# The end of layer 0: factor transposes among the last values' products, weight splits behind the values and behind six heads

## The chip, the cores and the metric

The kernel runs on one core of one Trainium2 chip. The metric is the device time in microseconds, the median of several runs. Before the change the median of three runs was 1199.51 us (1198.51 to 1203.9).

## What is computed

A transformer encoder of two layers over 512 tokens of width 1024, all in float32. Each layer is RMSNorm, a token mixer, a residual add, then RMSNorm, a squared-ReLU MLP of width 4096, a residual add; a final RMSNorm follows. Layer 0 mixes with dilated windows, layer 1 with differential attention. The change lies at the end of layer 0's mixer, which in the reference is:

```python
for (win, dil, nh) in A_GROUPS:          # ((128, 1, 6), (512, 4, 5), (2048, 16, 5))
    ...
    o, lse = lax.map(block_fn, (qb, starts))     # windowed softmax attention, o = p @ v
    glses.append(jax.nn.logsumexp(lse, axis=-1) - math.log(nh))
alpha = jax.nn.softmax(jnp.stack(glses, axis=-1), axis=-1)
o = jnp.concatenate([outs[g] * (n_groups * alpha[..., g])[..., None, None] ...], axis=2)
return o.reshape(B, S, A_HEADS * HEAD_DIM) @ w_o
```

So each of the 16 heads' outputs is multiplied, token by token, by a factor (its group's share, and here also one over its softmax sum), and the result is multiplied by the projection `w_o`.

## The kernel before

**Products in three parts.** Activations are kept with features on the partitions, 128 x 512 tiles. To hold float32 accuracy, each operand of a large product is split into a high half, rounded to the matmul's format by a copy on ScalarE (`whi`, L157, or `oh`, L693), and a low half, the rest, by a subtraction on VectorE (`wlo`, L158, or `ol`, L694). `mm3` (L168 to L170) then issues three products of 512 columns: high by high, high weight by low activation, low weight by high activation.

**Weights.** A unit of weights is 1024 x 256 and is fetched by SyncE into `raw`; its split is made in two halves of columns. `raw`, `whi` and `wlo` have two buffers each. `next_w()` hands out the unit fetched earlier and fetches and splits the one after it: one unit ahead. So the step that opens the last values splits the projection's first unit, and the step that opens the projection splits its second unit.

**Steps.** `linear_steps` is a generator: each `next` issues one `mm3` (one of eight blocks of the contraction), and after eight steps the result of one block of 128 output features, here one pair of heads, goes to `on_out`. `values0(j)` gives the values of pairs 2j and 2j + 1: for each pair 24 products into a bank `acc`, the scaling by VectorE (v, L554, remembered as `scaled`), four transposes (L557), the copy `vn` (L559), 16 small products with the probabilities (`o_ps`, L569), and the copy of the outputs `o` (L571). The end of layer 0 has `values0(2)`, pairs 4 and 5, and `values0(3)`, pairs 6 and 7.

**Factors.** `head_factors` computes the factors of all heads in `sA` with small VectorE steps and one exponential on ScalarE (L594 to L606). `factors(h0, h1)` transposes them on TensorE (L646), copies them to `fT` (L648) and writes them to the DRAM tile `fac` (L649). `spread` reads them back, broadcast over the partitions, into `fB` (L657, two DMAs for two pairs of heads). Heads 6 to 15 come first; heads 0 to 5 later, since their group's sums travel through DRAM to be reordered.

**Heads.** In the order `HEADS` = 3, 4, 5, 0, 1, 2, 6, 7 each pair's output is multiplied by its factors (L685), all but the first two behind the scaling of pair 7, and split to `oh` and `ol`. The tiles of `oh` reuse buffers that hold probabilities of the late heads. The projection takes the pairs in the same order: two banks for the first unit, then `linear_steps` for the other three units.

**Order.** The order of instructions on each engine is set when the kernel is compiled: a list scheduler takes them by program order as priority and by its own estimate of when each is ready. `high_priority` raises some, and `issue_after(ins)` places the instructions that a block issues on the engine of `ins` behind `ins`, on that engine alone. On the chip each engine then works through its queue in that order and waits on semaphores.

Of the kernel before, what the change touches and what calls it, by code (L numbers as in the profile page):

```python
# [23 lines left out]
KT = DM // P  # L24
# [42 lines left out]
def rev(ap):  # L67

    dims = [list(x) for x in ap.ap]
    off = ap.offset  # L70
    for d in dims[1:]:
        off += d[0] * (d[1] - 1)
        d[0] = -d[0]
    return bass.AP(tensor=ap.tensor, offset=off, ap=dims)
# [8 lines left out]
def tile_encoder(ctx: ExitStack, tc: tile.TileContext, x, rel_bias, gains, norm_final_g,  # L83
                 a_w_qkv, a_w_o, b_w_qkv, b_lambda, b_w_o, mlp_w_in, mlp_w_out, onehot, out):
    nc = tc.nc
    f32 = lambda t: t.bitcast(F32)
# [18 lines left out]
    def t_tile():  # L105
        return ps_t.tile([P, 512], F32, tag="t", name="t_ps")

    def o_tile():
        return ps_o.tile([P, 512], F32, tag="o", name="o_ps")
# [3 lines left out]
    def wide():  # L113
        wide_i.append(1)
        return acc_tile() if len(wide_i) % 5 in (0, 2) else s_tile()
# [30 lines left out]
    def fetch():  # L146
        if not units:
            return
        w, r0, kt, c0, ncol = units.pop(0)
        raw = wpool.tile([P, kt, ncol], F32, tag="raw", name="raw")  # L150
        n = 4 if w is b_w_o else 2
        hi = wpool.tile([P, kt, ncol], F32R, tag="whi", name="whi")
        lo = wpool.tile([P, kt, ncol], F32R, tag="wlo", name="wlo")
        fetched.append(nc.sync.dma_start(raw, w[r0:r0 + kt * P, c0:c0 + ncol].rearrange("(k p) c -> p k c", p=P)))
        for i in range(n):
            c = slice(i * ncol // n, (i + 1) * ncol // n)
            nc.scalar.copy(hi[:, :, c], raw[:, :, c])  # L157
            nc.vector.tensor_sub(lo[:, :, c], raw[:, :, c], f32(hi[:, :, c]))  # L158
        ready.append((hi, lo))

    def next_w():
        if not ready:
            fetch()
        fetch()
        return ready.pop(0)
# [8 lines left out]
    def linear_steps(ct0, kt, ncol, xs, on_out, bank=None, hooks=(), hold=None, order=None):  # L174

        hi, lo = next_w()
        xh, xl = xs
        hooks = dict(hooks)  # L180
        waiting = []
        n = 0
        for c in range(ncol // P):
            s = slice(c * P, (c + 1) * P)
            ps = (bank or acc_tile)()
            order = order or range(kt)
            for k in order:
                newest[0] = mm3(ps, hi[:, k, s], lo[:, k, s], xh[k], xl[k], k == order[0], k == order[-1])
                n += 1
                if n in hooks:  # L190
                    hooks.pop(n)()
                yield
            waiting.append((ct0 + c, ps))
            if hold is not None:
                hold.append((on_out, ct0 + c, ps))
                waiting = []
            elif not hooks:
                for a in waiting:
                    on_out(*a)
                waiting = []  # L200
        assert not waiting

    def run(steps):
        for _ in steps:
            pass
# [220 lines left out]
    def by_class(ap):  # L426
        return ap.rearrange("p (c m) -> p m c", c=4)

    def by_token(ap):
        return ap.rearrange("p (m c) -> p m c", c=4)  # L430
# [16 lines left out]
    for d in range(KT):  # L447
        split_first(d)
        for i, ps in enumerate(banks):
            _, _, hi, lo = first[i // 2]  # L450
# [93 lines left out]
    scaled = [None]  # L544

    def values0(j):
        def out_v(ct, ps):
            p = ct
            t = l0p.tile([P, SEQ], F32, tag="v0", name="v0", bufs=1)
            if p < 3:  # L550
                nc.vector.tensor_mul(t[:, 0:448], ps[:, 64:512], norm.rB[:, 64:512])
                nc.vector.tensor_mul(t[:, 448:512], ps[:, 0:64], norm.rB[:, 0:64])
            else:
                scaled[0] = nc.vector.tensor_mul(by_class(t), by_token(ps), by_token(norm.rB))  # L554
            T = t_tile()
            for b in range(NB):
                nc.tensor.transpose(T[:, b * P:(b + 1) * P], t[:, b * P:(b + 1) * P], ident)  # L557
            v = l0p.tile([P, NB, P], F32, tag="vn", name="vn", bufs=2)
            nc.scalar.copy(v.rearrange("p a b -> p (a b)"), T)  # L559

            ops = o_tile()
            for b in range(NB):
                for u in range(2 if p < 3 else 1):
                    for hh, rows in enumerate((lo64, hi64)):
                        if p < 3:
                            a, w, last = PT[2 * p + hh][:, 2 * b + u, :], v[:, (2 - b + u) % 4, rows], u == 1
                        else:
                            a, w, last = PT[2 * p + hh][:, b, :], v[:, 3 - b, rows], True
                        nc.tensor.matmul(ops[rows, b * P:(b + 1) * P], w, a, start=u == 0, stop=last)  # L569
            o = hpool.tile([P, SEQ], F32, tag=f"Bl{p}", name=f"o{p}")  # L570
            nc.scalar.copy(o, ops)  # L571
            O[p] = o

        yield from linear_steps(2 * j, KT, 256, norm.xs, out_v)
# [16 lines left out]
    def head_factors(al, parts):  # L591

        M = l0p.tile([P, NB, 1], F32, tag="fM", name="fM")
        nc.vector.tensor_reduce(M, al[:, :, :, 0], axis=AX.X, op=ALU.min)  # L594
        e = l0p.tile([P, NB, 3], F32, tag="fe", name="fe")
        nc.vector.tensor_sub(e, al[:, :, :, 0], M.broadcast_to([P, NB, 3]))
        nc.scalar.activation(e, e, AF.Exp, scale=-1.0)
        nc.vector.tensor_mul(e, e, al[:, :, :, 1])
        W = l0p.tile([P, NB, 1], F32, tag="fW", name="fW")
        nc.vector.tensor_reduce(W, e, axis=AX.X, op=ALU.add)  # L600
        nc.vector.reciprocal(W, W)
        nc.vector.tensor_scalar(W, W, 3.0, None, op0=ALU.mult)
        nc.vector.tensor_mul(e, e, W.broadcast_to([P, NB, 3]))
        for s, lo, hi, g in parts:
            nc.vector.reciprocal(s[:, :, lo:hi], s[:, :, lo:hi])
            nc.vector.tensor_mul(s[:, :, lo:hi], s[:, :, lo:hi], e[:, :, g:g + 1].broadcast_to([P, NB, hi - lo]))  # L606
# [35 lines left out]
    def factors(h0, h1):  # L642
        n = (h1 - h0) * NB
        with tc.high_priority():
            T = t_tile()
            mark = nc.tensor.transpose(T[0:n, 0:P], sA[:, h0:h1, :].rearrange("p h b -> p (h b)"), ident)  # L646
            fT = l0p.tile([40, P], F32, tag="fT", name="fT")
            nc.scalar.copy(fT[0:n], T[0:n, 0:P])  # L648
        nc.sync.dma_start(fac[h0 * NB:h1 * NB], fT[0:n])  # L649
        return mark  # L650
# [11 lines left out]
    head_factors(allS, [(sS, 0, 5, 1), (sS, 5, 10, 2)])  # L662

    run(values0(2))
    with tc.issue_after(newest[0].ins):
        turned = factors(6, 16)
    spread(3, 4)
    spread(5, 6)
    head_factors(allN, [(sN, 0, 6, 0)])
    last = values0(3)  # L670
    with tc.issue_after(turned.ins):
        for _ in range(KT):
            next(last)
    with tc.issue_after(newest[0].ins):
        turned = factors(0, 6)
# [5 lines left out]
    oh_, ol_ = {}, {}  # L681
    HEADS = (3, 4, 5, 0, 1, 2, 6, 7)
    for p in HEADS:
        with nullcontext() if p in (3, 4) else tc.issue_after(scaled[0].ins):
            nc.vector.tensor_mul(F[p], O[p], F[p])  # L685
        hi = hpool.tile([P, SEQ], F32R, tag=f"Bh{p}", name=f"oh{p}")
        lo = hpool.tile([P, SEQ], F32R, tag=f"Bl{p}", name=f"ol{p}")
        if p < 3:
            vh, vl, tv = rev(hi[:, :]), rev(lo[:, :]), F[p]
        else:  # L690
            vh, vl, tv = (rev(hi.rearrange("p (m c) -> p c m", c=4)), rev(lo.rearrange("p (m c) -> p c m", c=4)),
                          F[p].rearrange("p (c m) -> p c m", c=4))
        nc.scalar.copy(vh, tv)  # L693
        nc.vector.tensor_sub(vl, tv, f32(vh))  # L694
        oh_[p], ol_[p] = hi, lo

    def residual(nm):
        def on_out(ct, ps):
# [4 lines left out]
    nm = Norm(G_MLP0, "A")  # L703
    on = residual(nm)

    hi, lo = next_w()
    banks = [wide(), wide()]
    for p in HEADS:
        for c, ps in enumerate(banks):
# [389 lines left out]
```

## Time and profile before

| | before |
|---|---|
| median of three runs | 1199.51 us |
| lowest, highest | 1198.51, 1203.9 us |
| the profiled execution | 1198.23 us |
| its span, first to last instruction | 1196.3 us |
| granted TensorE clock, mean | 0.999 |
| TensorE (PE) busy | 1182.5 us, 99% |
| VectorE (DVE), ScalarE (ACT) busy | 628.6 us, 53%; 500.5 us, 42% |

PE is TensorE's products, PEld its weight loads, DVE VectorE, ACT ScalarE, SPq the queue from which SyncE issues transfers. Rows of a timeline give the start and the length in microseconds, the engine, the line of the kernel, the operation, the tile written and the tiles read, and in brackets how long the engine had been idle and what ended that. Products overlap in the array, so their rows are longer than the distance from one to the next. A row of a table of windows gives the window, its length, and each engine's busy time and number of instructions in it.

### The profile page before, as it was taken

Reading aid. Unit: us, or ns where it says so; the run is one execution under the profiler, and the core shown is the slowest. Engines: PE = TensorE matmul, PEld = TensorE weight load, DVE = VectorE, ACT = ScalarE, POOL = GpSimd, SP = SyncE. Lnnn points to the kernel's source line nnn. Section 1 sums busy time; section 2 is a strip of 40 time slices with the busy share of each in tenths; the row PEclk is TensorE's granted clock in tenths of the full one; section 3 lists DMA queues with packets and bytes.
Section 4 is the critical chain, followed back from the end, with each engine's and each line's share of the span. In section 5 each row is a group of like instructions: output and inputs, shape, how many; then the busy total and the mean of one; then the engine's idle time right before and its main releaser. Section 6 shows DMA issues by size and latency. Waiting matters only on the chain.

```text
span 1196.3 us, 14785 instructions
## 1 busy us (share of the span) xinstructions
PE 1182.5 (99%) x5888; PEld 989.5 (83%) x5888; DVE 628.6 (53%) x1056; ACT 500.5 (42%) x924; POOL 82.2 (7%) x141
## 2 busy tenths in 40 slices
PE   8999999999999999999999999999999999999997
PEld 6888877888888888888888898988888888888887
DVE  5875467554434434434458878676644344334323
ACT  6662345344323314323357666655444134223233
POOL 0000000100000000001101221223100000000012
PEclk9999999999999999999999999999999999999999
DMA  7722234323332333233423322312322332233211
GB/s 229 152 74 71 71 80 134 106 75 102 106 105 77 100 106 106 75 102 106 141 82 102 102 83 101 118 51 88 106 85 92 106 106 85 91 106 106 83 59 71
DMA packets 106698, 117.82 MB, mean 98 GB/s; under 512 B 4885, under 2 KB 97237, under 8 KB 106581
## 3 DMA queue, kind: packets, MB, share of 16 engines
q1 hardware_dynamic: 106566, 116.61, 31.0%
q8 instruction: 46, 0.75, 0.3%
q0 software_dynamic: 64, 0.27, 0.1%
q14 instruction: 22, 0.18, 0.0%
HBM read 114.60 MB, written 2.27 MB: 98 GB/s over the span
## 4 chain that ended last, share of the span: by engine, by line
PE 95%; DMA 2%; DVE 1%; ACT 1%; issue 1%; SPq 0%; POOL 0%; POOLq 0%; DVEq 0%; ACTq 0%
PE acc L169 15%; PE acc L170 15%; PE acc L168 15%; PE s_ps L169 14%; PE s_ps L170 14%; PE s_ps L168 14%; PE o_ps L944 2%; PE s_ps L361 1%; PE s_ps L360 1%; PE t_ps L935 1%; DMA fB<-fac 1%; PE o_ps L569 1%; PE s_ps L507 0%; PE t_ps L529 0%; DMA fd<-fsb 0%
## 5 line engine op out<-in xcount | busy, mean ns | idle before, releaser
L157 ACT CAST whi<-raw 128x1024 fp32r<-128x1024 f32 (+1 forms) x196 | 189.1, 1014 | 393.8 <-PE s_ps L169 205.3
L158 DVE TENSOR_TENSOR wlo<-raw,whi 128x1024 fp32r<-128x1024 f32 (+1 forms) x196 | 223.3, 1180 | 40.6 <-ACT whi L157 40.2
L168 PE MATMUL acc<-Ah,whi 128*128 128x512 f32 x472 | 185.4, 393 | 0.0
L170 PE MATMUL acc<-Ah,wlo 128*128 128x512 f32 x472 | 185.1, 392 | 0.0
L169 PE MATMUL acc<-Al,whi 128*128 128x512 f32 x472 | 184.6, 391 | 0.0
L168 PE MATMUL s_ps<-Ah,whi 128*128 128x512 f32 x352 | 137.0, 391 | 0.6 <-ACT whi L332 0.6
L169 PE MATMUL s_ps<-Al,whi 128*128 128x512 f32 x352 | 136.6, 390 | 0.0
L170 PE MATMUL s_ps<-Ah,wlo 128*128 128x512 f32 x352 | 136.3, 390 | 0.0
L169 PEld LDWEIGHTS acc<-Al,whi 128*128 128x128 f32 x472 | 88.7, 188 | 18.2 <-issue 0.2
L170 PEld LDWEIGHTS acc<-Ah,wlo 128*128 128x128 f32 x472 | 88.7, 188 | 18.2
L168 PEld LDWEIGHTS acc<-Ah,whi 128*128 128x128 f32 x472 | 88.7, 188 | 18.0 <-issue 0.2
L738 ACT ACTIVATE u<-u 128x512 f32<-128x512 f32 x64 | 40.0, 628 | 96.7 <-DVE u L737 96.7
L168 PEld LDWEIGHTS s_ps<-Ah,whi 128*128 128x128 f32 x352 | 65.9, 188 | 16.3 <-ACT whi L332 0.9
L747 DVE TENSOR_TENSOR h<-h,s_ps 128x512 f32<-128x512 f32 x33 | 22.7, 687 | 108.0 <-PE s_ps L170 108.0
L169 PEld LDWEIGHTS s_ps<-Al,whi 128*128 128x128 f32 x352 | 66.1, 188 | 13.6
L170 PEld LDWEIGHTS s_ps<-Ah,wlo 128*128 128x128 f32 x352 | 66.1, 188 | 13.5
L737 DVE SCALAR_TENSOR_TENSOR u<-s_ps,rB 128x512 f32<-128x512 f32 x38 | 26.3, 691 | 76.0 <-PE s_ps L170 73.8
L247 POOL TENSOR_TENSOR nacc<-nacc,nsq 128x512 f32<-128x512 f32 x18 | 25.9, 1438 | 530.1 <-ACT nsq L245 529.7
L168 PE MATMUL s_ps<-Bh,whi 128*128 128x512 f32 x152 | 59.1, 389 | 0.0
L169 PE MATMUL s_ps<-Bl,whi 128*128 128x512 f32 x152 | 59.1, 389 | 0.0
L170 PE MATMUL s_ps<-Bh,wlo 128*128 128x512 f32 x152 | 59.1, 389 | 0.0
L916 DVE CUSTOM_DVE_ANT_0 p<-s_ps,bias 128x512 f32<-128x512 f32 x64 | 43.3, 687 | 25.4 <-PE s_ps L361 17.8
(246 smaller groups left out, 2146.3 us busy)
## 6 DMA issues: line engine op xcount, KB each, us to landing
raw<-in_mlp_w_in_dram SPq DMA_DIRECT2D x32, 1024.0 KB, 5.3
raw<-in_mlp_w_out_dram SPq DMA_DIRECT2D x32, 1024.0 KB, 5.2
raw<-in_b_w_qkv_dram SPq DMA_DIRECT2D x12, 1024.0 KB, 5.2
raw<-in_a_w_qkv_dram SPq DMA_DIRECT2D x10, 1024.0 KB, 7.5
bias<-fd SPq DMA_DIRECT2D x16, 448.0 KB, 3.6
raw<-in_a_w_o_dram SPq DMA_DIRECT2D x4, 1024.0 KB, 5.2
raw<-in_b_w_o_dram SPq DMA_DIRECT2D x4, 1024.0 KB, 5.3
h<-in_x_dram SPq DMA_DIRECT2D x8, 256.0 KB, 4.0
```

Source lines behind the costliest of these rows:

```text
L157: nc.scalar.copy(hi[:, :, c], raw[:, :, c])
L158: nc.vector.tensor_sub(lo[:, :, c], raw[:, :, c], f32(hi[:, :, c]))
L168: nc.tensor.matmul(ps, ahi, bhi, start=first, stop=False)
L169: nc.tensor.matmul(ps, ahi, blo, start=False, stop=False)
L170: return nc.tensor.matmul(ps, alo, bhi, start=False, stop=last)
L247: eng.tensor_add(self.acc, self.acc, sq)
L360: nc.tensor.matmul(S, q[m][:, qs], k[m][:, ks], start=True, stop=False)
L737: nc.vector.scalar_tensor_tensor(u, ps, 0.0, nm.rB, op0=ALU.max, op1=ALU.mult)
L738: nc.scalar.activation(u, u, AF.Square)
L747: nc.vector.tensor_add(hT[ct], hT[ct], ps)
L916: nc.vector.tensor_tensor_reduce(out=xt, in0=S, in1=bias[h][m][:, b * P:b * P + SEQ], scale=1.0, scalar=3.0e38, op0=ALU.add, op1=ALU.min, ...
L944: marks["PV"] = nc.tensor.matmul(O[:, b, :], aT[:, k, :], v[:, k, es], start=k == 0, stop=k == NB - 1)
```

## The change

The last values are opened earlier in the program: their first two steps (the first of them with the fetch and the splits of the projection's first unit) now come ahead of the first transpose of factors. Of the steps, the first issues its VectorE work behind the scaling of pair 5. After the first transpose four steps follow instead of eight, and then the second transpose, so that it stands behind six steps of the last values and not behind eight. In the projection, the fetch and the split of the second unit are placed behind the splits of the sixth pair in `HEADS`, pair 2, on ScalarE and on VectorE; for that the loop over heads keeps the two instructions beside the tiles.

```diff
     run(values0(2))
+    last = values0(3)
+    with tc.issue_after(scaled[0].ins):
+        next(last)
+    next(last)
     with tc.issue_after(newest[0].ins):
         turned = factors(6, 16)
     spread(3, 4)
     spread(5, 6)
     head_factors(allN, [(sN, 0, 6, 0)])
-    last = values0(3)
     with tc.issue_after(turned.ins):
-        for _ in range(KT):
+        for _ in range(4):
             next(last)
     with tc.issue_after(newest[0].ins):
         turned = factors(0, 6)
...
-        nc.scalar.copy(vh, tv)
-        nc.vector.tensor_sub(vl, tv, f32(vh))
-        oh_[p], ol_[p] = hi, lo
+        oh_[p] = hi, nc.scalar.copy(vh, tv)
+        ol_[p] = lo, nc.vector.tensor_sub(vl, tv, f32(vh))
...
-    hi, lo = next_w()
+    with tc.issue_after(oh_[HEADS[5]][1].ins), tc.issue_after(ol_[HEADS[5]][1].ins):
+        hi, lo = next_w()
+    oh_, ol_ = ({p: t[0] for p, t in x.items()} for x in (oh_, ol_))
```

## The prediction

> **What bounds the kernel now.** I read the page's busy shares first, then the windows around the end of layer 0, then the queues of TensorE, VectorE, ScalarE and SyncE one by one in order of time.
>
> ```profile
> span 1196.3 us, 14785 instructions
> PE 1182.5 (99%) x5888; PEld 989.5 (83%) x5888; DVE 628.6 (53%) x1056; ACT 500.5 (42%) x924; POOL 82.2 (7%) x141
> ...
> PE 95%; DMA 2%; DVE 1%; ACT 1%; issue 1%; SPq 0%; POOL 0%; POOLq 0%; DVEq 0%; ACTq 0%
> ```
>
> TensorE is busy 99% of the span and carries 95% of the chain that ended last. An edit that takes no product away can only win back TensorE's idle time, so the question is how much of that lies in the stage that the diff touches.
>
> ```profile
> core 0: us, PE busy (x) PEld busy (x) DVE busy (x) ACT busy (x) POOL busy (x), PEclk, DMA share, GB/s
> ...
> 164.00:168.00 4.00, 2.60 (x29) 1.98 (x27) 3.08 (x7) 2.91 (x6) 0.00 (x0) 1.00 0.09 3
> 168.00:180.60 12.60, 12.60 (x69) 10.09 (x69) 5.64 (x13) 2.68 (x6) 0.00 (x0) 1.00 0.51 124
> 180.60:189.30 8.70, 7.30 (x54) 4.63 (x53) 7.48 (x10) 7.47 (x11) 0.00 (x0) 1.00 0.74 204
> 189.30:205.00 15.70, 15.70 (x69) 13.02 (x70) 10.54 (x14) 6.63 (x8) 0.37 (x1) 1.00 0.18 61
> ```
>
> There are two holes and no more: 4.00 - 2.60 = 1.40 us while the last values begin, and 8.70 - 7.30 = 1.40 us while the projection begins. Together 2.80 us, 0.23% of the span; that is the ceiling of what this diff can give here. The last window gives the price of one 512-column product in a full stretch: 15.70 / 69 = 0.2275 us. VectorE and ScalarE are nearly full (7.48 and 7.47 of 8.70) in the second hole, so there the order of their work decides.
>
> ```profile
> 166.07 0.66 PE L557 MATMUL t_ps<-ident,v 128*128 128x128 f32 x4 [1.40 <-DVE v L554]
> 166.56 0.27 PE L646 MATMUL t_ps<-ident,sA 128*40 128x128 f32 x1
> 166.76 1.09 PE L569 MATMUL o_ps<-pt,vn 128*64 128x128 f32 x16
> 167.79 0.50 PE L168 MATMUL acc<-Ah,whi 128*128 128x512 f32 x1
> ...
> 173.02 1.09 PE L569 MATMUL o_ps<-pt,vn 128*64 128x128 f32 x16
> ...
> 174.61 0.28 PE L646 MATMUL t_ps<-ident,sA 128*24 128x128 f32 x1
> ...
> 183.56 0.48 PE L168 MATMUL s_ps<-oh,whi 128*128 128x512 f32 x1
> ...
> 184.34 0.39 PE L169 MATMUL s_ps<-ol,whi 128*128 128x512 f32 x1
> 184.83 0.50 PE L168 MATMUL s_ps<-oh,whi 128*128 128x512 f32 x1
> ...
> 186.53 0.50 PE L170 MATMUL s_ps<-oh,wlo 128*128 128x512 f32 x1 [0.96 <-DVE wlo L158]
> ...
> 188.56 0.40 PE L168 MATMUL s_ps<-oh,whi 128*128 128x512 f32 x1
> 189.29 0.50 PE L169 MATMUL s_ps<-ol,whi 128*128 128x512 f32 x1 [0.33 <-DVE ol L694]
> ```
>
> The whole first hole stands in front of the transposes of pair 5's values: they wait for VectorE's scaling (v, L554), and the products of the last values, which were ready, are held behind the first factors' transpose at 166.56. The second hole ends at 189.29, when the low half `ol` of head pair 4 arrives. Between 183.56 and 188.56 TensorE lived on eight products with the projection's second weight unit (four of them L168/L169 pairs at 183.56 to 184.34 that lack their L170, since the unit's `wlo` was not there; two L170 and two L168 later).
>
> ```profile
> 168.03 1.22 DVE L158 TENSOR_TENSOR wlo<-raw,whi 128x1024 fp32r<-128x1024 f32 x1
> ...
> 170.63 0.20 DVE L606 TENSOR_TENSOR sA<-sA,fe 128x24 f32<-128x24 f32 x1
> ...
> 180.85 1.12 DVE L554 TENSOR_TENSOR v<-acc,rB 128x512 f32<-128x512 f32 x1 [3.62 <-PE acc L170]
> 181.80 1.87 DVE L685 TENSOR_TENSOR fB<-o,fB 128x512 f32<-128x512 f32 x3
> 184.65 0.69 DVE L685 TENSOR_TENSOR fB<-o,fB 128x512 f32<-128x512 f32 x1 [0.97 <-DMA fB<-fac]
> 185.25 2.35 DVE L158 TENSOR_TENSOR wlo<-raw,whi 128x1024 fp32r<-128x1024 f32 x2
> 187.52 1.71 DVE L694 TENSOR_TENSOR ol<-fB,oh 128x512 fp32r<-128x512 f32 x2
> ...
> 193.90 1.12 DVE L694 TENSOR_TENSOR ol<-fB,oh 128x512 fp32r<-128x512 f32 x1 [0.19 <-ACT oh L693]
> ```
>
> Here the reader sees why `ol` is late: ahead of it stand a wait of 0.97 us for the second spread of factors and 2.35 us of splits of that second unit.
>
> ```profile
> 169.36 0.21 ACT L597 ACTIVATE fe<-fe 128x12 f32<-128x12 f32 x1 [0.86 <-DVE fe L596]
> 174.16 0.59 ACT L571 COPY o<-o_ps 128x512 f32<-128x512 f32 x1 [4.59 <-PE o_ps L569]
> ...
> 175.65 0.32 ACT L648 COPY fT<-t_ps 24x128 f32<-24x128 f32 x1
> ...
> 180.92 2.00 ACT L157 CAST whi<-raw 128x1024 fp32r<-128x1024 f32 x2
> 183.11 1.67 ACT L693 CAST oh<-fB 128x512 fp32r<-128x512 f32 x2 [0.19 <-DVE fB L685]
> ...
> 187.03 0.64 ACT L693 CAST oh<-fB 128x512 fp32r<-128x512 f32 x1
> ```
>
> ```profile
> 141.41 12.96 SPq L154 DMA_DIRECT2D raw<-in_a_w_o_dram  x2
> ...
> 168.89 2.57 SPq L657 DMA_DIRECT2D fB<-fac  x4
> 176.00 0.30 SPq L649 DMA_DIRECT2D fac<-fT  x1
> 177.38 2.88 SPq L657 DMA_DIRECT2D fB<-fac  x4
> 180.37 7.67 SPq L154 DMA_DIRECT2D raw<-in_a_w_o_dram  x2
> ```
>
> **Part 1: two steps of the last values ahead of the first factors.** Six products, 6 x 0.2275 = 1.37 us, become free to run in a hole of 1.40 us. They need nothing that is late: their weights were split before 164, and their bank of `acc` is that of pair 4, whose scaling is over. Taken: -1.37 us; bounds -1.40 (the whole hole) and 0 (they are queued behind the transposes instead). The transpose at 166.56 waits for the same things as now, so the first spread stays; if the six were queued ahead of it outside the hole, its spread would land 1.37 us later, which feeds pair 3 alone, first used after 180.6: nothing.
>
> **The edge on the first unit's splits.** `issue_after(scaled)` binds only VectorE's two `wlo` splits of 1.22 us behind pair 5's scaling, and there they stand today, so the edge costs 0; without it they could stand ahead of the scaling and lengthen the hole by up to 2.4 us. Its matrix is fetched from 141.41 on; no DMA of the step lands later. As the step now precedes the second factors' arithmetic, the split at 168.03 may come out ahead of it entirely, with nothing lost.
>
> **Part 2: the second factors' transpose two steps earlier.** It stood behind 24 products; now it stands behind 18. TensorE reaches it at 167.79 + 12 x 0.2275 = 170.5, or at 171.6 if the 1.09 us of pair 5's outputs (173.02 now) are put ahead. Its input is ready at 170.63 + 0.20 = 170.83. So it waits 0 to 0.35 us; I take +0.2. Everything of the last values is queued behind it, and nothing else of weight. What follows it moves: the copy fT from 175.65 to about 171.2, into ScalarE's idle 4.59 us; the write to `fac` fits behind the first four spread issues, which end at 168.89 + 2.57 = 171.46 on SyncE; the four spread issues (2.88 us) and the third unit's load behind them go some 4.2 us earlier. POOL has nothing in this. The 0.97 us wait of VectorE for the spread is then gone, as VectorE comes to that multiplication at about 182.5 (181.80 + 1.87, less the 1.2 of parts 1 and 2) and the spread is in at about 180.4 (184.6 - 4.2). The load is not needed for another 15 us.
>
> **Part 3: the second unit's splits behind six heads.** ScalarE's 2.00 us at 180.92 go behind `oh` of pair 2 and VectorE's 2.35 us behind its `ol`. The low half that TensorE waits for at 189.29 then comes 0.97 + 2.35 = 3.32 us sooner against the start of the stretch. But TensorE loses its eight fillers (8 x 0.2275 = 1.82 us) and pair 7's outputs (1.09 us), which it did inside the wait and must do later: 3.32 - 1.82 - 1.09 = 0.41 us is what remains. Bounds: -1.40, the whole hole, and +0.6, if the low halves come only as much sooner as the two `wlo` take (2.35 us) and the fillers are all missed (2.35 - 1.82 - 1.09 = -0.56). Taken: -0.4. What is late next are the second unit's own splits: behind pair 2 they end at about 190, while TensorE, with the 28 products that then remain for six heads (6.4 us) and pair 7's outputs, is occupied from 184.8 (189.29 - 3.32 - 1.2) to 192.3. If that cover of 2 us were gone, each microsecond would cost one. Behind the splits in the queues stand pairs 6 and 7; their last low half ends at 193.90 + 1.12 = 195.0 today and should end near 193, by when TensorE has the second unit to work on.
>
> **The sum.** -1.37 + 0.2 - 0.4 = -1.6 us. The profiled execution took 1198.23 us, 1.93 more than its span, and the shown runs took 1198.51, 1199.51 and 1203.9; the profiled one lies 1.28 under their median and 0.28 under the fastest. 1198.23 - 1.6 = 1196.6, and 0.3 for a usual run: 1196.9.
>
> **The rivals.**
> *Both holes close (1195.8).* With pair 6's products done earlier, its transposes and outputs could fall inside pair 7's products, and `oh` of pairs 4 and 5, which reuse the buffers that these outputs read, could be made before the crowd on VectorE. Then -1.37 - 1.40 = -2.77, with the 0.3: 1195.8. Against it: VectorE still has six multiplications and seven low halves to do after pair 7's scaling.
> *The steps do not fall into the hole (1198.3).* The order on each engine comes from the compiler's own timing; if that has the scaling done earlier than the 166.07 here, the six products are placed behind the transposes: -0.4 + 0.2, 1198.3 with the 0.3.
> *The second transpose holds TensorE (1199.8).* It needs the exponential at 169.36 on ScalarE. In the new order the copy of pair 5's outputs (174.16 now) may stand ahead of it; then the factors come when pair 5's outputs are through and some 1.5 us of small steps (169.36 to 170.83) have followed, and at worst at 174.61 as today. TensorE would stand from 171.6 to 174.6: +3.0 - 1.37 - 0.4, giving 1199.8 with the 0.3. It is slower from 1.8 us of wait on, factors ready after 172.3 or 173.4. For it: everything behind that transpose is held. Against: the exponential has 4.59 us of idle ScalarE behind it.
> *Such a wait also costs clock (1205).* Were the 24 products of pair 7 at half speed after it, 24 x 0.2275 = 5.5 us come on top: 1205.3, just under 0.5% above the median before. The granted clock is 1.00 in every window above, right after a hole of 1.40 us, so nothing here bears it out.
> [...]
>
> **How the numbers follow.** Forecast 0.50 (its own range 1196.0 to 1198.0), both holes 0.18, not in the hole 0.18, transpose holds 0.11, clock 0.03. Low end: the ceiling of 2.80 off 1198.23 and half a microsecond of spread, 1194.9. High end: the third rival with the same spread, 1200.3. About 0.5% (6 us) is what a measurement of this kernel can tell from no change; the ceiling is under half of that, so faster by more needs something outside the stage (0.04), slower by more needs the clock case or a disturbed order later on (0.04).
>
> **What would show it.** Part 1: products of the last values start before the transposes of pair 5's values, and the 1.40 us in front of these are gone. Part 2: the 24-row transpose of `sA` starts near 170.9 and its spread lands before 181. Part 3: `wlo` behind the sixth `ol`, and no product with the second unit before 187. Wrong would be: a wait of over 1 us in front of the second transpose, or a new hole between 189 and 200 with `wlo` as its releaser.

## The result, and the profile after

The changed kernel took 1204.54 us (median of 12 runs, 1202.81 to 1209.17), the kernel before 1199.91 us beside it (12 runs, 1198.51 to 1203.96): ratio 1.0036 [1.0022, 1.005], 4.6 us slower. Forecast were 1196.9 us, at most 1200.3.

The first row of the changed kernel's page:

```profile
span 1205.6 us, 14785 instructions
```

This execution is 9.3 us longer than the profiled one before, but 5.16 of it arose before the stage begins (its first product, pair 7's first logits on L507, starts at 160.83 instead of 155.67), where every engine has the same instructions in the same order in both kernels; a weights load landed 23.45 us after its issue there, 19.1 before, and TensorE waited 2.07 us for what follows from it, not at all before. In one version below TensorE waited 2.8 us at this place, with the stage's begin at 162.31, and in another the stage begins at 161.22, so I do not put it down to the change; no run tests it. So I measure the stage by itself, from that product to the first sum of squares of the next norm: 82.72 us before, 86.98 after. These +4.26 us agree with the medians. After the stage 957.8 us follow, 957.9 before.

The stage in two windows, up to the projection's first product and from it on. Columns: window, length, busy time with the number of instructions for each engine, granted clock, DMA share, GB/s. Before:

```profile
155.67:180.65 24.98, 23.58 (x150) 19.15 (x150) 15.09 (x51) 9.86 (x31) 0.00 (x0) 1.00 0.39 101
180.65:238.39 57.74, 56.34 (x270) 45.27 (x269) 37.76 (x41) 27.23 (x37) 7.86 (x6) 1.00 0.39 120
```

After, with five windows of 3.41 us that are used below:

```profile
160.83:186.46 25.63, 23.32 (x150) 18.96 (x150) 15.15 (x51) 9.87 (x30) 0.00 (x0) 1.00 0.35 92
186.46:247.81 61.35, 57.69 (x271) 46.66 (x270) 38.05 (x41) 27.19 (x37) 7.76 (x6) 0.97 0.38 115
68.31:71.72 3.41, 3.41 (x11) 2.76 (x11) 3.38 (x12) 3.03 (x13) 0.00 (x0) 0.50 0.86 293
170.71:174.12 3.41, 1.63 (x21) 1.15 (x19) 1.17 (x4) 1.08 (x4) 0.00 (x0) 1.00 0.08 2
187.78:191.19 3.41, 1.92 (x22) 1.27 (x20) 1.88 (x4) 1.35 (x2) 0.00 (x0) 1.00 0.84 193
191.19:194.60 3.41, 1.23 (x4) 0.76 (x5) 2.85 (x5) 3.41 (x7) 0.00 (x0) 1.00 0.73 244
194.60:198.01 3.41, 3.41 (x19) 2.48 (x20) 3.41 (x6) 1.64 (x2) 0.00 (x0) 0.50 0.00 0
```

Up to the projection +0.65 us: TensorE's idle time rose from 1.40 to 2.31 there instead of vanishing. In the projection +3.61: idle time from 1.40 to 3.66, and 1.35 more of busy time, since the clock was at 0.50 for 3.41 us.

TensorE's rows after, in order of time:

```profile
170.41 0.40 PE L170 MATMUL acc<-Ah,wlo 128*128 128x512 f32 x1
170.65 0.60 PE L557 MATMUL t_ps<-ident,v 128*128 128x128 f32 x4
171.92 1.09 PE L569 MATMUL o_ps<-pt,vn 128*64 128x128 f32 x16 [0.68 <-ACT vn L559]
174.65 0.33 PE L557 MATMUL t_ps<-ident,v 128*128 128x128 f32 x1 [1.64 <-DVE v L554]
...
179.14 0.28 PE L646 MATMUL t_ps<-ident,sA 128*24 128x128 f32 x1
...
191.53 0.50 PE L168 MATMUL s_ps<-oh,whi 128*128 128x512 f32 x1 [1.83 <-ACT oh L696]
191.87 0.40 PE L168 MATMUL acc<-oh,whi 128*128 128x512 f32 x1
194.10 0.50 PE L169 MATMUL s_ps<-ol,whi 128*128 128x512 f32 x1 [1.84 <-DVE ol L697]
...
195.14 0.63 PE L170 MATMUL acc<-oh,wlo 128*128 128x512 f32 x1
195.56 0.63 PE L168 MATMUL s_ps<-oh,whi 128*128 128x512 f32 x1
```

The six products, the last of them at 170.41, were put ahead of pair 4's transposes (170.65), where there was no hole. The hole before pair 5's transposes is still there (1.64), with another of 0.68 before it. In the projection stand two waits of 1.83 and 1.84 us with two products between them, and behind them products 0.43 us apart instead of 0.23.

VectorE and SyncE after:

```profile
173.28 0.17 DVE L594 TENSOR_REDUCE fM<-allN 128x4 f32<-128x12 f32 x1 [2.21 <-DMA allN<-exS]
173.47 0.17 DVE L596 TENSOR_TENSOR fe<-allN,fM 128x12 f32<-128x12 f32 x1
173.56 1.03 DVE L554 TENSOR_TENSOR v<-acc,rB 128x512 f32<-128x512 f32 x1
174.44 2.34 DVE L158 TENSOR_TENSOR wlo<-raw,whi 128x1024 fp32r<-128x1024 f32 x2
...
177.71 0.20 DVE L606 TENSOR_TENSOR sA<-sA,fe 128x24 f32<-128x24 f32 x1
...
191.75 0.69 DVE L688 TENSOR_TENSOR fB<-o,fB 128x512 f32<-128x512 f32 x1 [1.34 <-DMA fB<-fac]
192.36 1.68 DVE L697 TENSOR_TENSOR ol<-fB,oh 128x512 fp32r<-128x512 f32 x2
```

```profile
176.77 2.57 SPq L657 DMA_DIRECT2D fB<-fac  x4
180.01 0.30 SPq L649 DMA_DIRECT2D fac<-fT  x1
183.70 3.00 SPq L657 DMA_DIRECT2D fB<-fac  x4
```

The second factors' first reduction (L594), ahead of pair 5's scaling in VectorE's queue, waits 2.21 us for a transfer, and the scaling waits with it. The scaling and both `wlo` splits then stand inside the second factors' arithmetic. And the second write to `fac` at 180.01 keeps SyncE from the next spread until 183.70. The chain before has that write in one row; after, the second row is the last read of that spread:

```profile
176.00 1.31 DMA fac<-fT
```

```profile
180.01 3.61 DMA fac<-fT
...
185.98 5.68 DMA fB<-fac
```

Counted from the stage's start, the write went out at 19.18 us instead of 20.33, 1.15 sooner. It took 2.30 us longer and the last read 0.79 longer (4.89 before, issued at 179.66), so that the spread landed at 30.83 instead of 28.88, 1.95 us later.

### The profile page after: what moved, and what is told of

Same layout as the page of the kernel before. It is cut to its first block, busy times and chain, and to the rows that moved or that the text cites. A ratio compares the mean times of both kernels' runs of the same rounds, so it can differ in the third digit from the quotient of the medians.

```text
span 1205.6 us, 14785 instructions
## 1 busy us (share of the span) xinstructions
PE 1186.9 (98%) x5888; PEld 993.4 (82%) x5888; DVE 629.3 (52%) x1056; ACT 500.5 (42%) x924; POOL 82.1 (7%) x141
## 4 chain that ended last, share of the span: by engine, by line
PE 93%; DMA 4%; DVE 1%; ACT 1%; issue 1%; SPq 0%; POOLq 0%; POOL 0%; DVEq 0%; ACTq 0%
PE acc L169 14%; PE acc L170 14%; PE acc L168 14%; PE s_ps L168 14%; PE s_ps L169 14%; PE s_ps L170 14%; DMA raw<-in_a_w_qkv_dram 2%; PE o_ps L948 2%; PE s_ps L361 1%; PE s_ps L360 1%; PE t_ps L939 1%; PE o_ps L569 1%; PE s_ps L507 0%; DMA fB<-fac 0%; PE t_ps L529 0%
```

## The experiments

Each was timed beside the kernel before on one chip; the stage is the profiled execution's. Medians of different groups are compared through the ratio, as the kernel before came to between 1199.9 and 1201.3 us.

**One part alone.** The changed kernel without the edges on the second unit, and the kernel before with these edges only:

```diff
-    with tc.issue_after(oh_[HEADS[5]][1].ins), tc.issue_after(ol_[HEADS[5]][1].ins):
-        hi, lo = next_w()
+    hi, lo = next_w()
```

> The change without the two edges on the second unit's splits. Stage = from the start of pair 7's 16 logit products (L507) to the 8 sum-of-squares products of the next norm (L252): 82.72 us before, 86.98 after. Theory A (the six products went ahead of pair 4's transposes, pair 5's scaling then stood on VectorE behind the wait for the second factors' sums, and with everything late the missing fillers and a cut clock did the rest): the late start stays, about 1 us, but fillers are back and the clock is not cut: stage 83.5 to 84.7, ratio 1.001 to 1.002. Rival B (the edges on the second unit alone carry the loss): 82.7 or less. Rival C (the moved steps carry it all): 86 to 87.

> The kernel before with only the edges on the second unit's splits. Theory A: the factors are on time, so the lost fillers (1.8 us) are about paid for by low halves that come sooner: stage 82.2 to 83.5, no cut clock. Rival B (the edges carry the loss): 85 to 87, with a window of granted clock under 0.95. Rival C: 82.7.

Measured: parts 1 and 2 alone 1203.47 us, 1.0028 [1.0014, 1.0042], stage 85.13 (27.17 up to the projection, 57.96 in it). The edges alone 1202.87 us, 1.0022 [1.0007, 1.0036], stage 86.78. Each loses by itself. In both the clock was cut, which theory A had not expected: the first lies above its range and under rival C's, the second in rival B's. In the run of the edges VectorE waits as in the changed kernel:

```profile
186.29 0.69 DVE L685 TENSOR_TENSOR fB<-o,fB 128x512 f32<-128x512 f32 x1 [1.32 <-DMA fB<-fac]
186.90 1.68 DVE L694 TENSOR_TENSOR ol<-fB,oh 128x512 fp32r<-128x512 f32 x2
```

Pair 2's multiplication starts 29.50 us into the stage there, before 28.98: it is bound by the landing of the spread, so the 0.97 us of waiting did not go with the splits but grew to 1.32. Part 2, which was to take this wait away, is not in this run, so only part 3's 2.35 us could be had. The two low halves that TensorE waits for came 1.74 us sooner (from 30.11 on instead of 31.85), against 1.82 + 1.09 us of work that TensorE no longer had for the wait.

**The six products in the hole.** The first two steps are issued on TensorE behind `tv[4]`, the last of pair 4's transposes of v; in the second run the edges are dropped as well:

```diff
-    with tc.issue_after(scaled[0].ins):
+    with tc.issue_after(tv[4].ins):
+        with tc.issue_after(scaled[0].ins):
+            next(last)
         next(last)
-    next(last)
```

> The change, with the first two steps of the last values issued on TensorE behind pair 4's transposes. Theory A: pair 5's scaling is again ahead of the wait for the second factors' sums, the six products fill the hole of 1.40 us, no cut clock: stage 80.9 to 81.9, that is 0.8 to 1.8 under before, which is the prediction's own sum. Rival B: 84 or more, since the edges are still there. Rival C (the earlier second transpose holds TensorE): a wait of over 1 us in front of it, 83 to 86.

> The same without the edges on the second unit's splits. Theory A: within 0.7 us of the run with them, 81.0 to 82.2. Rival B: at least 2 us under the run with them.

Measured: 1201.59 us, 1.0005 [0.9992, 1.0018], stage 83.90; without edges 1200.7 us, 0.9995 [0.9982, 1.0007], stage 84.54. The two windows of the first:

```profile
162.31:185.41 23.10, 23.03 (x146) 18.64 (x146) 15.30 (x51) 9.73 (x30) 0.00 (x0) 1.00 0.39 101
185.41:246.21 60.80, 58.03 (x274) 46.88 (x273) 37.98 (x41) 27.21 (x37) 7.76 (x6) 0.97 0.39 117
```

The hole is gone: 0.07 us idle up to the projection, 1.88 us won against before. But the projection then takes 3.06 us more than before, so that this version takes back most of the loss, not all of it, and the expected gain did not come.

**VectorE's order.** The second factors' softmax is issued behind pair 5's scaling:

```diff
-    head_factors(allN, [(sN, 0, 6, 0)])
+    with tc.issue_after(scaled[0].ins):
+        head_factors(allN, [(sN, 0, 6, 0)])
```

> The changed kernel with the second factors' softmax issued on VectorE behind pair 5's scaling (in the changed kernel its first reduction stood ahead of the scaling and waited 2.21 us for a transfer). Theory: the scaling starts as soon as its buffer and product are there, TensorE's 1.91 us pause ahead of pair 5's transposes falls to 0.9 to 1.3 us; the second factors get later by what the scaling and two low halves take (1.0 + 0.6), so that the second transposes are no sooner; stage 86.0 to 87.0, time 1203.5 to 1204.5, the clock still cut behind the waits for oh and ol. Rival (VectorE's order does not matter, the buffer of v sets the time): pause 1.8 to 2.0 us, stage 86.8 to 87.2.

Measured: 1202.31 us, 1.0007 [0.9994, 1.0019], stage 86.79. TensorE's and SyncE's order is the changed kernel's here, and on ScalarE only the exponential of these factors moved. The pause before pair 5's transposes is gone entirely (expected were 0.9 to 1.3 left) and the projection starts at 23.92 instead of 25.63, 1.06 sooner than before. So the scaling held behind the waiting reduction is what kept the hole open:

```profile
167.46 1.06 DVE L554 TENSOR_TENSOR v<-acc,rB 128x512 f32<-128x512 f32 x1 [0.22 <-PE t_ps L557]
...
170.61 0.16 DVE L594 TENSOR_REDUCE fM<-allN 128x4 f32<-128x12 f32 x1
```

The version with the hole filled has the reduction behind the scaling too (174.75 and 171.61 there). Of the 2.53 us that it wins up to the projection against the changed kernel (25.63 to 23.10) VectorE's order alone gives 1.71; the place of the six products gives the other 0.82, mostly the wait of 0.68 us ahead of pair 4's outputs. The profiled stage is as long as the changed kernel's since the projection took 62.87 us here, with the clock cut for two windows. By the medians, 1.0007 against the changed kernel's 1.0036, VectorE's order alone takes back most of the loss.

**The clock.** 11 and 11 transposes of the unit matrix, read by nobody, (`turning(after, n)` issues n of them behind `after`) keep TensorE at work in the two waits of the changed kernel; 8 and 11 in those of the version with the hole filled; 7 and 11 in those that the edges alone open:

```diff
+            if p == HEADS[0]:
+                idle = turning(turn_v[7], 11)
...
+        idle = turning(m, 11)
```

> The changed kernel with 22 more transposes of the unit matrix that nothing reads: 11 behind pair 7's transposes, 11 between the two products of the second head's high half and its other four, so that TensorE is at work in both of its waits (1.83 us for oh, 1.84 us for ol) with 11 x 0.16 = 1.76 us each. Theory (the waits themselves cost 3.7 us, and on top the clock is cut behind them, so that products stand 0.43 us apart instead of 0.23 for some 1.5 us in all): granted clock 1.00 from 189 to 205, stage 85.2 to 85.7 (86.98 in the changed kernel), time 1202.7 to 1203.4 (1204.5). Rival 1 (the wide spacing of the products is not the idle time's doing: the operands come late one by one): spacing of 0.43 us stays, stage 86.9 to 87.3. Rival 2 (the transposes themselves delay what follows): stage over 87.3.

> The version whose first two steps stand behind pair 4's transposes (stage 83.90, before 82.71), with 8 and 11 transposes of the unit matrix in its two waits (1.52 and 1.92 us). Theory (clock cut is 1.3 of its loss): stage 82.4 to 82.8, time 1200.0 to 1200.6, that is no loss against the kernel before, and granted clock 1.00 in the stage. Rival (clock cut is not from the idle time): stage 83.8 to 84.2, time 1201.3 to 1202.

> The kernel before with the two edges alone (measured: stage 86.78 with two cuts of the clock, 1202.87 against 1200.65), and with 7 and 11 transposes of the unit matrix in the two waits that they open (1.1 us for oh, 1.8 for ol). Theory (the edges lose 1 to 2 us by the eight products that no longer fill the waits, and the rest by the clock): granted clock 1.00 in the stage, stage 83.7 to 84.7, 1200.6 to 1201.8 with before at 1200. Rival (all the loss is the clock): stage 82.5 to 83.2, no slower than before. Second rival (the clock has nothing to do with the waits): stage over 86.

Measured: in the changed kernel 1204.16 us, 1.0026 [1.0011, 1.0042], stage 86.79, a miss. With the hole filled 1199.74 us, 0.9989 [0.9979, 1.0], stage 82.57, as expected. The edges alone 1201.69 us, 1.0011 [0.9998, 1.0023], stage 85.01 (86.78), above the expected 84.7; the last read of its spread landed 30.36 us into the stage, without the transposes 29.41. In these three runs the later waits no longer cost clock: from the projection's first product on it was granted at 1.00, where without the transposes it came to 0.97, 0.97 and 0.94. In the first, the cut came behind the earlier pair of waits (at 170 in the changed kernel) instead. Its two windows, and two of the run with the hole filled but no transposes:

```profile
168.15:171.56 3.41, 1.59 (x21) 1.11 (x19) 1.14 (x4) 1.04 (x4) 0.00 (x0) 1.00 0.08 2
171.56:174.97 3.41, 2.88 (x10) 2.44 (x11) 3.27 (x8) 1.08 (x3) 0.00 (x0) 0.50 0.02 6
```

```profile
189.21:192.62 3.41, 0.84 (x3) 0.41 (x4) 2.46 (x4) 3.41 (x6) 0.00 (x0) 1.00 0.90 281
192.62:196.04 3.42, 3.42 (x14) 2.38 (x16) 3.42 (x5) 2.36 (x3) 0.00 (x0) 0.50 0.03 12
```

So in these runs it is TensorE's idle time in the waits that costs the clock. All cuts in the stage last 3.41 us (nine runs), or twice that (three). In the changed kernel cuts begin at 68.31, 194.60 and 1201.53: 126.29 and 1006.93 us apart, which is 37 and 295 times 3.4133. So the cuts of this execution lie on a grid of 3.413 us. With such a grid laid through the cuts of each of the 18 profiled executions, the stage's windows agree: each with 1.60 us of TensorE work or less was followed by a window at 0.50 (twelve windows, of 0.19 to 1.60 us, the highest with VectorE's edge alone and the write first, below), and none with 1.63 or more started a cut (1.63 is the window of 170.71 above, 1.59 that of the run with transposes). A cut window with 2.67 us of work or less was followed by a second one (2.41, 2.60 and 2.67), one with 2.88 or more was not. The border is not sharp to 0.03 us: at the end of the run with the hole filled, outside the stage, a window of 1.59 us (from 1196.14 on) was not followed by a cut. The profile models the ends of products.

Where the grid falls differs from one execution to the next: in two runs of one order of instructions, the version with the hole filled and no edges, the cuts begin 31.29 and 30.18 us into the stage. So whether a pair of waits costs clock depends on that too. Sliding the grid over the traces in 20 steps, an estimate: the changed kernel has a window under 1.61 at every position and 1.55 on the mean, parts 1 and 2 alone 0.3, the version with the hole filled 0.55 and, without its edges, 1.0, the kernel before none, and that with the hole filled and the transposes none.

**The late write.** First the write of the second factors went out on GpSimd's queue, in the version with the hole filled:

```diff
-        nc.sync.dma_start(fac[h0 * NB:h1 * NB], fT[0:n])
+        (nc.gpsimd if h0 == 0 else nc.sync).dma_start(fac[h0 * NB:h1 * NB], fT[0:n])
```

> The version whose first two steps stand behind pair 4's transposes, with the 12 KB write of the second factors issued on GpSimd's queue instead of SyncE's. There the write took 3.5 us from issue to the spread's issue (1.31 in the kernel before), with the four spread reads of the first factors in flight. Theory A (it waits behind those reads because it is in the same queue): under 2 us to landing, second spread 1.5 to 2.2 us sooner, VectorE's wait for fB shorter by as much, waits for oh and ol together 3.4 down to 1.5 or less, stage 81.8 to 82.8, time 1199.5 to 1200.5. Theory B (the 16 DMA engines are busy with the reads, whatever the queue): 3 us or more again, stage 83.7 to 84.4, time 1201.2 to 1202.

Measured: 1204.05 us, 1.0022 [1.0012, 1.0033], stage 85.95. The write took 3.56 us against 3.43 from SyncE's queue (rows of the two chains, SyncE's first). That is theory B for the landing; the stage lies above both ranges, as TensorE waited 2.29 us for `oh` (1.25 with the hole filled) and the clock was cut for two windows.

```profile
179.32 3.43 DMA fac<-fT
...
185.11 4.96 DMA fB<-fac
```

```profile
176.28 3.56 DMA fac<-fT
```

In both runs the write was reported near the landing of the last of the four reads ahead of it, from whichever queue: 20.44 and 20.89 us into the stage, that read at 21.20 and 20.72. What ties the two together no run shows.

Then the spread of pairs 5 and 6 was to go behind that write. A move in the program alone changed no engine's order (the next run is the version with the hole filled once more); with an edge to the write, two reads are ahead of it instead of four:

```diff
-    spread(5, 6)
...
+    with tc.issue_after(wrote[0].ins):
+        spread(5, 6)
```

> The version whose first two steps stand behind pair 4's transposes (stage 83.90), with the spread of pairs 5 and 6 (two of the four reads of the first factors) issued behind the write of the second factors instead of ahead of it. In six traces this write landed 5.0 to 5.7 us (once 6.5) behind the last read issued ahead of it, as late as that read itself. Theory: it now waits only for the reads of pairs 3 and 4 (issued at +12.8 and +13.5 from the stage's start), lands at +18.0 to +18.7 (+20.1 without the move), the last read of the second spread is issued at +20.0 to +20.9 (+22.4) and lands 1.5 to 2.3 us sooner; VectorE's wait for fB ahead of pair 2's multiplication (1.02 us) is gone, the two waits for oh and ol sum to 2.0 to 2.6 (3.44), the clock is cut less or not at all, stage 81.5 to 82.7, time 1199.2 to 1200.4. Rival A (the eight reads share the same 16 DMA engines, so that the last lands as late whatever the order): last landing under 0.7 us sooner, stage 83.3 to 84.1. Rival B (pairs 5 and 6 are now late themselves): VectorE waits for fB ahead of pair 5's multiplication, stage over 84.

> The version whose first two steps stand behind pair 4's transposes (stage 83.90 and, measured again, 84.23), now with an edge that holds the spread of pairs 5 and 6 behind the issue of the second factors' write in SyncE's queue; two reads are in flight ahead of the write instead of four. Theory: the write lands with the reads of pairs 3 and 4 at +18.0 to +18.7 from the stage's start (+20.0 in those runs), the last read of the second spread is issued at +20.3 to +21.0 (+22.2 to +22.4) and lands 1.3 to 2 us sooner; VectorE's wait for fB ahead of pair 2's multiplication is under 0.3 us, the waits for oh and ol sum to 2.0 to 2.8 (3.44 and 3.88), stage 81.8 to 83.2, time 0.5 us above the kernel before to 0.8 below it. Rival A (eight reads share the same 16 DMA engines, so that the last lands as late whatever the order): under 0.7 us sooner, stage 83.6 to 84.3. Rival B (pairs 5 and 6 become late): VectorE waits for fB ahead of pair 5's multiplication, stage over 84.3.

Measured: the move alone 1202.18 us, 1.0018 [1.0005, 1.0032], stage 84.23; the same order of instructions gave 1.0005 above, which shows what such intervals leave open. With the edge 1200.18 us, 0.9996 [0.9979, 1.0013], stage 82.17. Its chain:

```profile
174.10 2.21 DMA fac<-fT
...
178.67 5.96 DMA fB<-fac
```

The write took 2.21 us instead of 3.43, so with two reads ahead of it instead of four it was sooner by 1.22 us, though here it was reported 1.27 us behind the second of its two reads. But the last read took 5.96 instead of 4.96 and landed only 0.2 us sooner in the stage (27.57 against 27.76), as rival A had it for the landing. This landing differs by up to 1.6 us between two runs of one order. Over the six with the hole filled and four reads ahead it came 27.56 to 29.12 us into the stage, over the four with two reads ahead 26.72 to 27.84, so the order wins some 0.7 us on the mean. The 1.7 us of stage come mostly from a clock that stayed at 1.00 in this execution (1.5 us less of busy time, 0.2 less of idle time); with about 0.5 cut windows on the mean by the same estimate, that was chance.

**Fillers.** Only VectorE's edge is kept, so that eight products with the second unit's high half stand ahead of the wait; or no edge; or both edges with 6 and 8 transposes in the waits.

```diff
-    with tc.issue_after(oh_[HEADS[5]][1].ins), tc.issue_after(ol_[HEADS[5]][1].ins):
+    with tc.issue_after(ol_[HEADS[5]][1].ins):
```

> As the run with the write ahead of the reads, and of the two edges that hold the second unit's splits only VectorE's is kept, so that the high half of the weights is there early and eight products with it stand between the first heads' products and pair 7's outputs. Theory (the products fill the waits for oh and ol, 8 x 0.23 = 1.82 us of 2.0 to 2.6): waits under 1 us in all, no cut of the clock, stage 80.3 to 81.6, time 1198.0 to 1199.3, faster than the kernel before by 0.6 to 1.9. Rival (the splits on ScalarE ahead of oh delay the high halves by as much, 2 x 0.6 us): stage 81.6 to 82.7, as without the edge.

> As the run with the write ahead of the reads, without both edges on the second unit (its splits stand where the kernel before has them: on VectorE between pair 2's multiplication and the low halves, two of 1.2 us). Theory: fillers as in the run that keeps VectorE's edge, but the low halves 2.4 us later, so one wait of 1.5 to 2.7 us for wlo or ol; stage 81.0 to 82.5, time 1198.7 to 1200.2, that is within 1 us of the run with both edges, and later than the run with VectorE's edge alone by 0.5 to 1.5. Rival (the edges carry the loss whatever comes ahead of them): stage 80.0 to 80.9, the fastest of the three.

> As the run m4, with VectorE's edge alone on the second unit: eight products with its high half stand ahead of pair 7's outputs. In the run labelled m3 (the same with four reads ahead of the write) they stood ahead of one wait of 3.68 us, with the clock cut behind it, stage 84.20. Theory: the sooner landing takes 1 to 1.8 us of that one wait, which stays above 1.5; stage 82.2 to 83.4, time within 0.8 us of the kernel before. Rival (that wait is set by ScalarE's two splits and copies, not by the spread): wait 3.3 us or more, stage 83.9 to 84.4.

> As the run m4, without both edges on the second unit, whose low halves (two of 1.2 us on VectorE) then stand ahead of the low halves of the heads; with four reads ahead of the write this gave stages of 84.54 and 83.09 with one wait of 2.3 to 3.9 us. Theory: pair 2's multiplication no longer waits (it waited little there: 27.21 against 25.67 plus 0.6, that is 0.9 us), so everything behind it is 0.5 to 1 us sooner, stage 82.0 to 83.3, time within 1 us of the kernel before. Rival (VectorE's two low halves of the weights set the wait): stage 83.1 to 84.5 again.

> As the run m4, with 6 and 8 transposes of the unit matrix in the two waits. Theory (a sooner spread and no cut clock together): granted clock 1.00 in the stage, stage 81.2 to 82.3, 0.3 to 1.5 us below the kernel before, and below the run k2 (stage 82.57, ratio 0.9989). Rival (the spread lands no sooner): stage 82.4 to 83, as k2.

In the first two the write was behind four reads after all, so they do not test what was expected of them, and the second is the version without edges once more. Measured, in this order: 1.0013 [0.9999, 1.0026], stage 84.20; 1.0010 [0.9998, 1.0023], 83.09; then with the write ahead of two reads 0.9986 [0.9973, 0.9998], 82.51; 0.9988 [0.9971, 1.0005], 82.57; 0.9999 [0.9982, 1.0015], 82.49. With VectorE's edge alone and the write first, 1199.65 us against 1200.2, the kernel is the only one whose interval lies under 1; among sixteen versions one such interval can come by chance. Differences between these last three are not settled. In the last, both edges with transposes, the spread landed at 27.84 and the stage is in the rival's range. In all versions with the hole filled the projection starts 1.8 us sooner and then takes 1.3 to 3.7 us longer than before (59.04 to 61.43 us against 57.74; 62.82 with the write on GpSimd's queue): the start is won and the wait for the factors takes it back.

The rows of the highest window that was followed by a cut, in the run with VectorE's edge alone and the write first:

```profile
184.22:187.63 3.41, 1.60 (x20) 0.99 (x18) 3.41 (x7) 3.31 (x6) 0.00 (x0) 1.00 0.90 274
187.63:191.05 3.42, 3.42 (x19) 2.41 (x20) 3.42 (x4) 1.73 (x3) 0.00 (x0) 0.50 0.00 1
```

## Why the prediction was wrong

- **The ceiling** (2.80 us of idle time) held, and no version passed it. What was missing was that idle time can also grow: from 2.80 to 5.97 us, and with it TensorE's busy time by 1.09, from the cut clock.
- **The sum, as measured.** Up to the projection +0.65 us, where -1.17 was forecast; the low half's wait and the work done later +1.91, where -0.4 was forecast (part 3 below); the clock +1.70, where nothing was forecast: 4.26 together. Behind the product that waits for the low half, the projection takes 53.71 us against 49.10: 2.91 of these 4.61 are the eight products and pair 7's outputs, and 1.70 is half of the window of 3.41 us at half clock.
- **The base.** 1198.23 + 0.3 for a usual run is 1.4 us under the 1199.91 of the twelve runs before. So the forecast lay 3.0 under them while its parts gave 1.6.
- **Part 1, -1.37 us.** That products of the last values can close the hole is right; the order on two engines is wrong. Placed behind pair 4's transposes, with the scaling ahead of the reduction on VectorE, the six products close the hole and the projection starts 1.88 us sooner. The sentence that they "become free to run in a hole" assumed the compiler would put them there; the bound "0 (they are queued behind the transposes instead)" left out the third place, ahead of pair 4's transposes. The larger step that failed stands behind "there they stand today, so the edge costs 0": it took the order around the scaling on VectorE to stay as it was. The sentence that without the edge the splits could lengthen the hole looked at the wrong neighbour: what got ahead of the scaling on VectorE was the second factors' reduction and its 2.21 us of waiting, shown by putting it behind.
- **The split that "may come out ahead of it entirely, with nothing lost"**: the scaling, 1.03 us, and both splits, 2.34, came out inside the second factors' arithmetic, so the factors were ready at 177.91, 7.1 us later on the clock (1.9 us later in the stage) and not at 170.83.
- **Part 2, "the write to `fac` fits behind the first four spread issues"**: it did in the queue, but its landing waited for the four reads, 3.61 us instead of 1.31. Forecast was that TensorE reaches the second transpose 3.7 us sooner (170.9), that the second spread goes 4.2 us sooner and that VectorE's 0.97 us wait vanishes. TensorE reached it 0.63 us sooner (18.31 us into the stage, 18.94 before) and did not wait there, where 0.2 was taken; the spread landed 1.95 us later, and the wait became 1.34. In the version with the hole filled the spread came 1.1 us sooner.
- **Part 3, -0.4 us.** Failed is "0.97 + 2.35 = 3.32 us sooner". In the changed kernel the product that waits for the low half starts 7.64 us behind the projection's first (194.10 and 186.46), before 8.64: 1.00 us sooner. The splits did go from VectorE's queue there, but the late spread took most of it back. Against the lost 2.91 us that makes +1.91. In the run of the edges alone 1.74 instead of 2.35 were won, which makes +1.2; with the clock kept up by transposes the stage is still 2.3 us over before, outside the bound of +0.6. That the second unit's splits are covered was right: no product waited for its `wlo`, and the new waits are for `oh` and `ol`.
- **The rival with 0.03** was near in kind: a wait that costs clock. That its 1205 is near the measured time is luck: it was priced at 24 products, 5.5 us, after one wait of 3.0 us at the transpose, where none arose; what came was one window of 3.41 us, 1.70, behind two waits of 1.8 us. No run shows the clock at half for 24 products: the cuts in the stage last one window of 3.41 us or two. The rival's dismissal, by a clock of 1.00 right after a hole of 1.40 us, took that hole by itself, where the cuts followed the work in a window: 1.23 us in the window of 191.19, and 2.01 in the emptiest window of the stage before.

## What to carry to other kernels

Price a move by where the order on every engine's queue puts it, including what waits for a transfer ahead of the work that frees the hole: here that wait on VectorE cost more (1.71 us) than the place of the moved products on TensorE (0.82). Where idle time is spread over short waits, add it up over any stretch of 3.4 us: here 1.60 us of work or less in a window of 3.41 us was followed by 3.41 us at a clock of 0.50, and two waits of 1.83 and 1.84 us cost clock by coming close together, where holes of 1.40 and 0.96 us, 20 us apart, cost none. A small write followed by a dependent read is priced with the reads in flight ahead of it: here 12 KB took 1.31 us with none and 3.43 behind four, 3.56 from another queue. And a start won upstream of a transfer that lands no sooner turned into a wait here: 1.88 us won up to the projection, 3.06 lost in it.

## What was not expected of the hardware

- The clock's windows: 3.41 us, on one grid in the changed kernel's execution (37 and 295 windows from cut to cut), in the stage cut behind 1.60 us of work or less, not behind 1.63 or more.
- A 12 KB write: 1.31 us with no read in flight, 3.43 and 3.61 behind four reads of 256 KB, 2.21 behind two, 3.56 behind four from another queue. Over all versions with the hole filled the next spread went out 3.28 to 4.24 us behind the write with four reads ahead and 1.75 to 2.45 with two, 1.38 before.
- Nineteen transposes that nobody reads, put into the waits, kept the clock up: 83.90 and 84.23 to 82.57 us in the stage, ratio 1.0005 and 1.0018 to 0.9989. In the version with the write first, fourteen brought nothing that the timing shows (0.9996 to 0.9999).
